# A first head pair projected side by side, and bias reads and stores issued by POOL

## The chip, the core and the metric

The kernel runs on one core of a Trainium2 chip. Five engines work side by side and wait for each other through semaphores: TensorE (PE in the profile; its weight loads are PEld), VectorE (DVE), ScalarE (ACT), GpSimd (POOL) and SyncE (SP). Transfers between main memory (DRAM) and the on-chip memory are issued by an engine's queue and carried out by 16 DMA engines that all queues share. The metric is device time in microseconds, median of several executions. Before the change it is 973.29 us (three runs, 971.8 to 973.51).

## The reference

One inference step of a two-layer encoder on 288 tokens at once: 256 of a prompt and 32 of a sample that has cached keys and values. The model width is 1024, everything is float32. Cut to its order:

```python
for layer in range(2):
    h = rmsnorm(x, g_mix[layer])
    if layer == 0:   # 16 heads of 64 from one projection
        qa, ka, va, qb, kb, vb = proj_ab(h, w_in_ab)
        o = merge_heads(chunk_band_attn(qa, ka, va, rel_bias_a),   # 8 heads, bias by clipped distance
                        stick_break(qb, kb, vb))                   # 8 heads, no softmax
    else:
        q, k, v, log_f = proj_c(h, w_in_c, b_f_c)                  # 16 heads
        o = forget_attn(q, k, v, log_f)                            # logits + cumulative log forget
    x = x + o @ w_out[layer]
    x = x + memory_attn(rmsnorm(x, g_xattn[layer]), *memory_kv(mem_prompt, ...), w_xq, w_xo)
    x = x + swiglu(rmsnorm(x, g_ffn[layer]), w_gate, w_up, w_down)
y = rmsnorm(x, g_final)
```

Besides y, the keys and values of both layers, those of the memory tokens and the log forget values are outputs. In the banded attention of layer 0 a frame reads its own chunk of 64 and the chunks before it; the bias of head h for query i and key j is a table entry at the distance i - j, clipped at 128.

## The kernel before

**Layout.** Activations lie transposed: eight blocks `x[k]` of 128 features by 288 tokens. Weights come in units of 128 x 1024 float32 (512 KB), one unit giving 128 output features: eight 128 x 128 blocks, one for each block of x. Each number is kept as a rounded part and a remainder (`hi`, `lo` for weights; `hh`, `hl` for activations), and `mm3` makes each product of three TensorE instructions, hi x hh, hi x hl and lo x hh. A unit's projection is thus 24 matrix products over 288 columns, summed in one PSUM bank.

**Units.** `unit(src)` (line 132) takes one of four buffers `st`, has SP load the unit, ScalarE copies it to `hi` (line 141) and VectorE subtracts to get `lo` (line 142). There are five buffers for `hi` and four for `lo`. `project` runs a unit's 24 products into a bank of tag `pj` (four banks, `acc`) and then calls `tick()`. Small work, attention above all, uses four further banks of tag `at` (`att`).

**Ticks.** Attention, norm scales and the preparation of memory tokens are generators in the list `active`. Each `tick()` lets each of them run to its next `yield`, so that their instructions stand between two projections. `Next.scale` has the columns of the norm (`Norm.columns`: sums of squares on TensorE, then eleven small VectorE instructions for the inverse root), a `yield`, and then the rows (`Norm.rows`: TensorE spreads the scale over the partitions, ScalarE copies it to `rstd`). A projection's result is multiplied by `rstd` when it leaves PSUM; projections that end before `rstd` is there hold their bank and wait in the list `waiting`.

**The start.** SP loads the first unit in three parts between the four pieces of x. ScalarE and VectorE scale and split each block of x by the gain (`split_scaled`, lines 247 and 250), and the first unit's products follow block by block. Keys and values are loaded as whole units. `pairs` then runs over eight head pairs: `proj(j)` projects queries, keys and values, the pair's attention is made active, after each second pair that of the sample too, and `memory.steps` puts projections of the memory tokens between.

**The bias of layer 0.** `rel_lines` makes a line of 384 biases per head, writes it to DRAM, and eight DRAM to DRAM copies (line 745) repeat it 128 times with a step of 385, so that a read with a step of 384 is the line shifted by one per row. `rel_prompt` reads two rectangles per head from this (lines 755 and 756), and POOL fills the masked corners. `softmax` adds the bias on VectorE (line 350); the transposes at lines 374 to 376 follow on TensorE. In layer 1 POOL builds the bias (lines 901 to 904) from the cumulative sums, which SP reads back from DRAM (`ck`, line 896).

**Orders.** A planner at compile time sets each engine's order from the order of the code and from when it expects operands to be ready; on the chip each engine then works strictly in that order and waits where an operand is late. SP issues every transfer: weights, x, bias reads, stores of keys and values (line 730), of memory keys (553) and values, of the forget values (848, 849) and of y (976).

## Time and profile before

| | |
|---|---|
| median of three runs | 973.29 us |
| the profiled execution | 974.15 us, of which 972.3 us are the span from first to last instruction |
| granted TensorE clock, mean | 0.995 |
| busy: TensorE, VectorE, ScalarE, POOL | 955.3, 588.6, 484.8, 195.1 us |
| matrix products on TensorE | 7495 |
| moved by DMA | 163.59 MB, 168 GB/s on the mean |

A row of a timeline gives the start and the length in microseconds, the engine, the line, the operation and what it writes and reads; in brackets stands how long the engine was idle before it and what ended that. `SPq` is SP's queue: the row tells when a transfer is issued, not when it lands. Rows of the chain of waits give start, length and what the end of the program hung on at that moment. A row of stretches gives, for a part of the span, each engine's busy time and number of instructions, the granted clock of TensorE and what the DMA engines did. Neighbouring matrix products overlap in the records, so that the distance of their starts, not their length, is what one costs.

### The profile page before, as it was taken

What the parts mean: (1) busy time and instruction counts of PE and PEld (TensorE: products, weight loads), DVE (VectorE), ACT (ScalarE), POOL (GpSimd) and SP (SyncE); (2) the same over time, 40 slices, a digit from 0 to 9 for tenths busy, and PEclk for the clock granted to TensorE, in tenths of its full rate; (3) what the DMA queues carried; (4) which work ended last, traced back from release to release, by engine and by line L of the source; (5) the groups of instructions that cost most, each with busy time, mean ns of one, the idle gap of its engine ahead of it and who ended that gap; (6) DMA issues with size and microseconds to landing.
All of it is one profiled execution on the core that took longest, in us unless ns stands there. A gap on an engine that the chain in (4) does not pass through costs nothing.

```text
span 972.3 us, 19122 instructions
## 1 busy us (share of the span) xinstructions
PE 955.3 (98%) x7495; PEld 923.2 (95%) x7495; DVE 588.6 (61%) x1133; ACT 484.8 (50%) x856; POOL 195.1 (20%) x291
## 2 busy tenths in 40 slices
PE   8999999999999999999999999999999999999997
PEld 7889999998999999999998999999989999999996
DVE  6587555676666555754565666657757655555452
ACT  5456768545554444444444545446546544444331
POOL 3021001310213222411004333213002222222010
PEclk9999999999999999999999999999999999999999
DMA  7775455544254444554555555555434444444431
GB/s 232 247 241 189 137 180 181 183 162 147 103 174 154 173 162 164 191 192 160 173 202 161 179 190 191 169 164 179 150 117 159 159 159 173 163 164 173 165 117 49
DMA packets 59721, 163.59 MB, mean 168 GB/s; under 512 B 8192, under 2 KB 20528, under 8 KB 59632
## 3 DMA queue, kind: packets, MB, share of 16 engines
q1 hardware_dynamic: 59632, 162.38, 49.0%
q8 instruction: 59, 0.97, 0.4%
q14 instruction: 30, 0.25, 0.1%
HBM read 152.20 MB, written 11.72 MB: 169 GB/s over the span
## 4 chain that ended last, share of the span: by engine, by line
PE 91%; DMA 3%; DVE 3%; issue 1%; ACT 1%; SPq 1%; POOL 0%; DVEq 0%; POOLq 0%; ACTq 0%
PE pj L68 51%; PE dn L68 14%; PE op L68 11%; PE mv L68 5%; PE po L68 1%; PE xo L68 1%; PE xs L68 1%; DMA st<-w_ab 1%; PE zb L68 1%; PE sc L68 1%; DVE lo L142 1%; DMA skew<-lined 1%; DMA x<-xT 1%; PE xss L68 1%; PE xt L614 0%
## 5 line engine op out<-in xcount | busy, mean ns | idle before, releaser
L141 ACT CAST hi<-st 128x1024 fp32r<-128x1024 f32 x260 | 272.2, 1049 | 335.7 <-issue 147.3
L68 PE MATMUL pj<-hh,hi 128*128 128x288 f32 (+1 forms) x1352 | 406.3, 301 | 0.0
L68 PE MATMUL pj<-hl,hi 128*128 128x288 f32 (+1 forms) x1352 | 399.9, 296 | 1.7 <-DVE hl L250 1.7
L68 PE MATMUL pj<-hh,lo 128*128 128x288 f32 (+1 forms) x1352 | 400.2, 296 | 0.0
L142 DVE TENSOR_TENSOR lo<-st,hi 128x1024 fp32r<-128x1024 f32 x260 | 322.7, 1242 | 127.4 <-PE dn L68 41.2
L68 PEld LDWEIGHTS pj<-hh,hi 128*128 128x128 f32 x1352 | 257.0, 190 | 5.8 <-issue 4.2
L68 PEld LDWEIGHTS pj<-hl,hi 128*128 128x128 f32 x1352 | 257.1, 190 | 3.3 <-DVE hl L250 3.2
L68 PEld LDWEIGHTS pj<-hh,lo 128*128 128x128 f32 x1352 | 256.9, 190 | 0.0
L68 PE MATMUL dn<-fh,hi 128*128 128x288 f32 x400 | 108.5, 294 | 0.0
L68 PE MATMUL dn<-fh,lo 128*128 128x288 f32 x352 | 103.3, 294 | 0.0
L68 PE MATMUL dn<-fl,hi 128*128 128x288 f32 x304 | 89.5, 294 | 0.0
L68 PE MATMUL op<-ol,hi 128*128 128x288 f32 x256 | 75.8, 297 | 0.0
L68 PE MATMUL op<-oh,hi 128*128 128x288 f32 x256 | 75.5, 297 | 0.0
L68 PE MATMUL op<-oh,lo 128*128 128x288 f32 x256 | 75.2, 294 | 0.0
L68 PEld LDWEIGHTS dn<-fh,hi 128*128 128x128 f32 x400 | 72.3, 188 | 0.0
L68 PEld LDWEIGHTS dn<-fh,lo 128*128 128x128 f32 x352 | 66.2, 188 | 0.0
L213 POOL TENSOR_TENSOR ssq<-ssq,sq 128x288 f32<-128x288 f32 (+1 forms) x37 | 37.7, 1018 | 119.8 <-ACT sq L202 76.8
L68 PEld LDWEIGHTS dn<-fl,hi 128*128 128x128 f32 x304 | 57.1, 188 | 0.0
L695 POOL TENSOR_TENSOR fl<-us,fh 128x288 fp32r<-128x288 f32 x38 | 32.9, 865 | 119.3 <-ACT fh L694 119.3
L690 DVE TENSOR_TENSOR us<-pj,rstd 128x288 f32<-128x288 f32 x44 | 20.1, 457 | 59.9 <-PE pj L68 59.9
L691 POOL TENSOR_TENSOR gs<-gs,sg 128x288 f32<-128x288 f32 x44 | 38.9, 884 | 75.8 <-ACT sg L689 75.8
L68 PEld LDWEIGHTS op<-ol,hi 128*128 128x128 f32 x256 | 48.2, 188 | 0.6 <-issue 0.4
(257 smaller groups left out, 1204.9 us busy)
## 6 DMA issues: line engine op xcount, KB each, us to landing
st<-w_gate SPq DMA_DIRECT2D x44, 512.0 KB, 3.3
st<-w_up SPq DMA_DIRECT2D x44, 512.0 KB, 3.2
st<-w_down SPq DMA_DIRECT2D x44, 512.0 KB, 3.2
st<-w_c SPq DMA_DIRECT2D x25, 512.0 KB, 3.3
st<-w_ab SPq DMA_DIRECT2D x23, 512.0 KB, 4.4
st<-w_xk SPq DMA_DIRECT2D x16, 512.0 KB, 3.4
st<-w_xv SPq DMA_DIRECT2D x16, 512.0 KB, 3.5
st<-w_xq SPq DMA_DIRECT2D x16, 512.0 KB, 3.5
```

Of the source, the lines that this page charges most:

```text
L68: T.matmul(out, lhsT, rhs, start=start, stop=stop, skip_group_check=True)
L141: S.copy(hi[:, b], st[:, b])
L142: V.tensor_tensor(lo[:, b], st[:, b], hi[:, b].bitcast(F32), ALU.subtract)
L213: eng.tensor_tensor(s[:, :self.n], self.acc[i][:, :self.n], q[:, :self.n], ALU.add)
L690: V.tensor_tensor(us, pu[:, :NT], cur.r, ALU.mult)
L691: G.tensor_tensor(gs, gs, sg, ALU.mult)
L695: G.tensor_tensor(lo, us, hi.bitcast(F32), ALU.subtract)
```

## The change

- The first pair's three units are loaded in parts (256, 256 and 512 columns), part by part between the pieces of x, and split into hi and lo as the parts arrive. `side_by_side` runs, for each block of x, the three products of queries, keys and values, into three banks (one of tag `at`, two of tag `pj`), and calls `tick()` once, where the three projections before called it three times.
- The columns of the first norm come at the first tick, right after those 72 products, and the rows two ticks later, after the second unit of pair 1. The first pair's attention in layer 0 is held back by two ticks, in layer 1 by one (`later`).
- POOL's queue issues what concerns the bias of layer 0 (the line, its copy to DRAM, the skew, the reads) and the stores of keys, values, memory keys, memory values and forget values. SP keeps the loads of weights, x, caches and memory tokens, the read back of the cumulative sums, and the store of y.
- The line is made at the start. The skewed copy has 64 rows a head for 128 and is written by two transfers of four heads for eight of one. The bias of a head is one tile of 128 x 256 for 128 x 384: the later query half has its keys 0 to 255, the earlier half uses columns 128 to 255, and one corner is masked. The tiles come from the general pool of token tiles, and a pair's reads are issued ahead of its projections.
- y is stored in three transfers for six.

```diff
-    first = wp.tile([P, 1024], F32, tag="st", bufs=4, name="first")
-    def first_part(c0, c1):
-        DMA.dma_start(first[:, c0:c1], a["w_ab"][0][:, c0:c1])
-    first_part(0, 256)
+    first = [wp.tile([P, 1024], F32, tag="st", bufs=4, name=f"first{i}") for i in range(3)]
+    def first_part(i, c0, c1):
+        DMA.dma_start(first[i][:, c0:c1], a["w_ab"][4 * i][:, c0:c1])
+    PARTS = ((0, 256), (256, 512), (512, 1024))
+    first_part(0, *PARTS[0])
     for i in range(4):
         DMA.dma_start(xh[i], a["xT"][:, 2 * i * NT:2 * (i + 1) * NT])
         if i == 0:
             DMA.dma_start(gain, a["gains"])
-            first_part(256, 512)
-        if i == 1:
-            first_part(512, 1024)
+        if i < 3:
+            for u in range(3):
+                if i or u:
+                    first_part(u, *PARTS[i])
...
+    SKEW = 64 * 385
+    line = cst.tile([8, 384], F32, name="line")
+    lined = dr.tile([8, 384], F32, name="lined")
+    skew = dr.tile([8, SKEW], F32, name="skew")
+    G.dma_start(line[:, 128:384], a["rel"][:, 0:256])
...
+    G.tensor_copy(line[:, 0:128], line[:, 128:129].to_broadcast([8, 128]))
+    G.dma_start(lined, line)
+    for h in range(0, 8, 4):
+        G.dma_start(bass.AP(tensor=skew.tensor, offset=skew.offset + h * SKEW, ap=[[SKEW, 4], [385, 64], [1, 384]]),
+                    bass.AP(tensor=lined.tensor, offset=lined.offset + 384 * h, ap=[[384, 4], [0, 64], [1, 384]]))
...
-    def unit(src, st=None, pieces=1):
-        if st is None:
-            st = wp.tile([P, 1024], F32, tag="st", bufs=4, name=name("st"))
-            DMA.dma_start(st, src)
-        hi = wp.tile([P, 1024], F32R, tag="hi", bufs=5, name=name("hi"))
-        lo = wp.tile([P, 1024], F32R, tag="lo", bufs=4, name=name("lo"))
-        for c in range(pieces):
-            b = slice(c * 1024 // pieces, (c + 1) * 1024 // pieces)
-            S.copy(hi[:, b], st[:, b])
-            V.tensor_tensor(lo[:, b], st[:, b], hi[:, b].bitcast(F32), ALU.subtract)
-        return hi, lo
+    def unit_tiles():
+        return [wp.tile([P, 1024], F32R, tag=t, bufs=n, name=name(t)) for t, n in (("hi", 5), ("lo", 4))]
+    def split_weights(st, w, c0=0, c1=1024):
+        hi, lo = (t[:, c0:c1] for t in w)
+        S.copy(hi, st[:, c0:c1])
+        V.tensor_tensor(lo, st[:, c0:c1], hi.bitcast(F32), ALU.subtract)
+    def unit(src):
+        st = wp.tile([P, 1024], F32, tag="st", bufs=4, name=name("st"))
+        DMA.dma_start(st, src)
+        w = unit_tiles()
+        split_weights(st, w)
+        return w
...
-    def project(src, h, n=NT, w=None, begun=None):
-        if begun:
-            w, p = begun
-        else:
-            w, p = w or unit(src), acc("pj")
-        with tc.issue_after(warmed.ins):
-            for k in range(BEGIN if begun else 0, KT):
-                mm3(p[:, :n], w, k, h, k, k == 0, k == KT - 1)
+    def project(src, h, n=NT, begun=None):
+        w, p = begun or (unit(src), acc("pj"))
+        for k in range(BEGIN if begun else 0, KT):
+            mm3(p[:, :n], w, k, h, k, k == 0, k == KT - 1)
         tick()
         return p
...
+    def store(dst, t):
+        G.dma_start(dst, t)
...
-            if self.gi != 1:
+            if self.gi > 1:
                 yield 1
             y = self.norm.columns()
             yield 1
+            if self.gi == 0:
+                yield 1
             p = self.norm.rows(y)
...
+                b0 = at[i] if at else c0
+                V.tensor_tensor_reduce(out=out[:, c0:c1], in0=s[:, c0:c1], in1=bias[:, b0:b0 + c1 - c0], scale=-1.0, scalar=3e38,
...
-                DMA.dma_start(a["mkT"][l, i], t[:, 0:NP])
+                store(a["mkT"][l, i], t[:, 0:NP])
...
-                        DMA.dma_start(a["mv"][l, t, :, hd * 256:hd * 256 + 256], v[:, 0:NP])
+                        store(a["mv"][l, t, :, hd * 256:hd * 256 + 256], v[:, 0:NP])
...
-    def rel_lines():
-        ln = cst.tile([8, 384], F32, name="line")
-        DMA.dma_start(ln[:, 128:384], a["rel"][:, 0:256])
-        V.tensor_copy(ln[:, 0:128], ln[:, 128:129].to_broadcast([8, 128]))
-        d = dr.tile([8, 384], F32, name="lined")
-        DMA.dma_start(d, ln)
-        sk = dr.tile([8, 128 * 385], F32, name="skew")
-        for h in range(8):
-            DMA.dma_start(bass.AP(tensor=sk.tensor, offset=sk.offset + h * 128 * 385, ap=[[385, P], [1, 384]]),
-                          bass.AP(tensor=d.tensor, offset=d.offset + 384 * h, ap=[[0, P], [1, 384]]))
-        return sk
-    def rel_rows(sk, h, c, rows, n):
-        return bass.AP(tensor=sk.tensor, offset=sk.offset + h * 128 * 385 + c, ap=[[384, rows], [1, n]])
-    def rel_prompt(sk, h):
-        t = wk.tile([P, 384], F32, tag="bi", bufs=5, name=name("bi"))
-        DMA.dma_start(t[:, 0:128], rel_rows(sk, h, 256, P, 128))
-        DMA.dma_start(t[:, 128:384], rel_rows(sk, h, 128, P, 256))
-        G.memset(t[0:64, 64:128], NEG)
-        G.memset(t[0:64, 320:384], NEG)
+    def rel_rows(h, c, rows, n):
+        return bass.AP(tensor=skew.tensor, offset=skew.offset + h * SKEW + c, ap=[[384, rows], [1, n]])
+    def rel_prompt(h):
+        t = tok("bi")
+        G.memset(t[0:64, 192:256], NEG)
+        G.dma_start(t[0:64, 0:192], rel_rows(h, 128, 64, 192))
+        G.dma_start(t[64:128, 0:256], rel_rows(h, 64, 64, 256))
         return t
 
-    def rel_sample(sk, g):
+    def rel_sample(g):
         t = wk.tile([P, 384], F32, tag="bi", bufs=5, name=name("bs"))
         for h in range(4):
-            DMA.dma_start(t[32 * h:32 * h + 32, 0:160], rel_rows(sk, 4 * g + h, 128, NS, 160))
+            G.dma_start(t[32 * h:32 * h + 32, 0:160], rel_rows(4 * g + h, 128, NS, 160))
...
+        def side_by_side():
+            p = [att("pj"), acc("pj"), acc("pj")]
+            with tc.issue_after(warmed.ins):
+                for k in range(KT):
+                    for u in range(3):
+                        mm3(p[u][:, :NT], w0[u], k, cur.h, k, k == 0, k == KT - 1)
+            tick()
+            return p
+        biases = {}
         def proj(j):
+            if j < 4:
+                biases[j] = [rel_prompt(2 * j + i) for i in range(2)]
             b = 12 * (j // 4) + j % 4
             kv = 8 * (j // 4) + j % 4
-            qs[j] = evac_q(cur, project(w[b], cur.h, w=w0 if j == 0 else None))
-            if j == 0:
-                proj.line = rel_lines()
-            ks[j] = evac_kv(cur, project(w[b + 4], cur.h), a["kv0"][kv])
-            vs[j] = evac_kv(cur, project(w[b + 8], cur.h), a["kv0"][kv + 4])
-        def attend(j):
+            p = side_by_side() if j == 0 else (project(w[b + 4 * i], cur.h) for i in range(3))
+            p = iter(p)
+            qs[j] = evac_q(cur, next(p))
+            ks[j] = evac_kv(cur, next(p), a["kv0"][kv])
+            vs[j] = evac_kv(cur, next(p), a["kv0"][kv + 4])
+        def attention(j):
             args = (qs[j], ks[j], vs[j], vns, j)
             if j < 4:
-                return attend_prompt(*args, [rel_prompt(proj.line, 2 * j + i) for i in range(2)], o[0][j], o[1][j])
+                return attend_prompt(*args, biases.pop(j), o[0][j], o[1][j], (128, 0))
             return stick_prompt(*args, o[0][j], o[1][j])
+        def attend(j):
+            return later(attention(j), 2) if j == 0 else attention(j)
...
+    def later(g, n):
+        for _ in range(n):
+            yield 1
+        yield from g
...
-        DMA.dma_start(a["lf"][0:256].rearrange("(t p) h -> p t h", p=P), lf[:, 0:32].rearrange("p (t h) -> p t h", h=H))
-        DMA.dma_start(a["lf"][256:288], lf[0:NS, 32:48])
+        G.dma_start(a["lf"][0:256].rearrange("(t p) h -> p t h", p=P), lf[:, 0:32].rearrange("p (t h) -> p t h", h=H))
+        G.dma_start(a["lf"][256:288], lf[0:NS, 32:48])
...
-            return attend_prompt(qs[j], ks[j], vs[j], vns, j, bias, o[0][j], o[1][j])
+            return later(attend_prompt(qs[j], ks[j], vs[j], vns, j, bias, o[0][j], o[1][j]), j == 0)
...
-    w0 = None
+    w0 = [unit_tiles() for _ in first]
     for m in range(KT):
         cur.block(m, start=True)
-        if m == 1:
-            w0 = unit(None, first, 4)
+        if m in (1, 3, 5):
+            for st, w in zip(first, w0):
+                split_weights(st, w, *PARTS[m // 2])
...
-            DMA.dma_start(a["y"][P * t:min(P * t + P, NT), b], out[r, b])
+        DMA.dma_start(a["y"][P * t:min(P * t + P, NT)], out[r])
```

11 lines of the change are left out of this document (5 added, 6 removed).

## The prediction

> **What bounds the kernel now.** I read the page first: the span and the engines' shares of it.
>
> ```profile
> span 972.3 us, 19122 instructions
> PE 955.3 (98%) x7495; PEld 923.2 (95%) x7495; DVE 588.6 (61%) x1133; ACT 484.8 (50%) x856; POOL 195.1 (20%) x291
> ```
>
> TensorE is the bound nearly everywhere, and the change removes none of its matrix products. So whatever it can win lies in the 17 us in which TensorE was idle and in the stretches in which it was busy but slow. Next I cut the span into stretches around its gaps; columns are length, then busy time and instruction count of PE, PEld, DVE, ACT and POOL, the granted clock, the DMA share and GB/s.
>
> ```profile
> 5.10:17.10 12.00, 10.30 (x36) 8.72 (x36) 10.91 (x20) 8.48 (x17) 4.82 (x6) 1.00 0.76 273
> 17.10:31.70 14.60, 14.60 (x115) 14.03 (x114) 7.04 (x19) 3.16 (x6) 1.17 (x8) 1.00 0.90 248
> 31.70:34.10 2.40, 0.38 (x4) 0.14 (x2) 2.15 (x12) 1.83 (x8) 0.00 (x0) 1.00 0.60 198
> 34.10:37.60 3.50, 3.48 (x16) 3.09 (x16) 1.52 (x5) 1.94 (x4) 0.00 (x0) 0.51 0.52 156
> 62.90:65.00 2.10, 1.19 (x7) 0.64 (x6) 2.10 (x8) 1.53 (x4) 0.80 (x1) 1.00 0.99 292
> 80.00:100.00 20.00, 19.88 (x172) 18.60 (x172) 12.99 (x31) 12.25 (x20) 2.91 (x2) 1.00 0.52 178
> 522.10:524.00 1.90, 0.20 (x3) 0.03 (x1) 1.19 (x7) 1.46 (x7) 0.89 (x3) 1.00 0.08 20
> 525.60:529.10 3.50, 3.50 (x17) 3.50 (x16) 0.78 (x1) 0.29 (x1) 0.00 (x0) 0.51 0.53 142
> ```
>
> A healthy stretch is 80 to 100: TensorE idle 0.12 us of 20. Against it stand four losses. The start: 12 us hold 36 products. Two idle gaps of 2.0 us (2.40 - 0.38) and 1.7 us (1.90 - 0.20), each followed by about 3.4 us at a granted clock of 0.5, in which half the work is done: another 1.7 us each. A smaller gap of 0.9 us (2.10 - 1.19) at 62.9. What a product costs shows in the starts of successive ones, early and late:
>
> ```profile
> 5.13 0.61 PE L68 MATMUL pj<-hh,hi 128*128 128x288 f32 x1
> 6.08 0.61 PE L68 MATMUL pj<-hl,hi 128*128 128x288 f32 x1 [0.34 <-DVE hl L250]
> 11.68 0.61 PE L68 MATMUL pj<-hl,hi 128*128 128x288 f32 x1 [1.08 <-DVE hl L250]
> ...
> 14.49 0.44 PE L68 MATMUL pj<-hh,hi 128*128 128x288 f32 x1
> 14.73 0.44 PE L68 MATMUL pj<-hl,hi 128*128 128x288 f32 x1
> ...
> 18.02 0.30 PE L68 MATMUL pj<-hh,hi 128*128 128x288 f32 x1
> 18.15 0.29 PE L68 MATMUL pj<-hl,hi 128*128 128x288 f32 x1
> ```
>
> They follow each other by 0.24 us in the first 17 us and by 0.13 us afterwards. Early TensorE is slow and also waits for x: the first product starts at 5.13, the second at 6.08.
>
> The gap at 31.7 I followed through the chain of waits, then through SP's and VectorE's timelines.
>
> ```profile
> 16.27 6.79 DMA skew<-lined
> 23.14 6.50 DMA st<-w_ab
> 39.73 0.84 PE po L68 x8
> ```
>
> ```profile
> 13.74 5.05 SPq L745 DMA_DIRECT2D skew<-lined  x8
> 22.72 0.32 SPq L756 DMA_DIRECT2D bi<-skew  x1
> 23.14 1.21 SPq L136 DMA_DIRECT2D st<-w_ab  x1
> ...
> 30.80 1.23 DVE L142 TENSOR_TENSOR lo<-st,hi 128x1024 fp32r<-128x1024 f32 x1 [2.97 <-ACT hi L141]
> 31.95 0.28 DVE L350 CUSTOM_DVE_ANT_0 e<-sc,bi 128x128 f32<-128x128 f32 x1
> ```
>
> SP issues in order. It spent 5.05 us on the eight skew copies; then the bias reads wait for those copies to land, and behind a bias read stands the next weight load, issued only at 23.14 and landed 6.50 later. ScalarE splits it, VectorE splits it at 30.80, and behind VectorE's split waits the softmax of the first pair (31.95), whose result the transposes on TensorE need at 31.7 and lack until 33.9. SP's order makes this gap, not bandwidth: SP waits while weights could flow.
>
> **The change, part by part.** The sum is made against the profiled execution, 974.15 us, 0.86 above the median of 973.29.
>
> First pair side by side. TensorE gets nine products per block of x in place of three while x arrives. Bytes: three weight units (1.57 MB), x (1.18 MB) and the gains are 2.8 MB, as much as is moved today by 13 us, only in another order:
>
> ```profile
> GB/s 0 0 0 0 0 19 186 203 173 269 358 286 256 79 53 131 232 275 366 352 336 347 314 339 288 311 336 440 439 410 416 416 403 303 189 63 25 0 0 0
> DMA packets 1456, 2.80 MB, mean 215 GB/s; under 512 B 296, under 2 KB 560, under 8 KB 1456
> ```
>
> So the last of x comes at about 12.5, or later with the skew copies beside it; I take 13.5. ScalarE, VectorE and SP do the same work cut finer (five more issues of 0.4 to 0.6 us, before x's last piece). TensorE: busy without gaps from 6.1 us. Today it turns fast at 17.0, 5.3 us after the last gap (before 11.68); with gapless work from 6.1, I let it turn at 11.0 (bounds 10 and never). That is some 23 products by 11.0 and 49 more at 0.13, thus 17.4; from the supply, 13.5 + 1.0 for the scaled copies + 18 x 0.13 = 16.8. I take 18.2 for the pair, 0.8 above the later of these because the second and third unit's first parts are split one after another while TensorE waits; bounds 17.2 and 22.7 (slow throughout: 6.1 + 69 x 0.24).
>
> Rows of the norm later. The order becomes pair 0, norm columns, two units of pair 1, norm rows, third unit. Prices:
>
> ```profile
> 18.82 1.40 PE L68 MATMUL nrm<-mean,ssq 128*128 128x2 f32 x12
> ...
> 23.33 0.75 PE L68 MATMUL nr<-ident,y 128*128 128x128 f32 x6
> ...
> 24.12 0.40 ACT L280 COPY rstd<-nr 128x288 f32<-128x288 f32 x1 [5.61 <-PE nr L68]
> 24.92 0.81 DVE L729 TENSOR_TENSOR kv<-pj,rstd 128x288 f32<-128x288 f32 x2
> ...
> 27.18 0.27 PE L332 MATMUL vt<-ident,kv 128*128 128x128 f32 x1
> 28.46 0.40 PE L68 MATMUL pj<-hh,hi 128*128 128x288 f32 x1
> ```
>
> Columns 1.4, rows 0.75. The third unit must wait for a bank: four "pj" banks hold k and v of pair 0 and two units of pair 1, and the first is free after the rows, the copy to rstd and two evacuations, the second of them the first of the two at 24.92 (0.45 each): about 25.3, 1.3 us after the rows end at 24.08. Queued behind this wait on TensorE is everything else; nothing hides it. It is the new stall. After: 18.2 + 1.4 + 48 x 0.13 + 0.75 + 1.3 + 24 x 0.13 = 31.0; the transposes of v with the scores (1.28, from 27.18 to 28.46) and the transposes of the weights (0.75) make 33.0. Today the same work stands done at 39.7 (39.73 in the chain above). Gain 6.7, bounds 2.2 (pair done at 22.7) and 7.7. The gap and slow clock at 31.7 are in it: skew and bias no longer pass SP, and weight loads run four buffers ahead.
>
> First attention two steps later. Its transposes and those of pair 1's values fall into one step and share four banks: a one-off loss of 0.7 (0 to 1.5; the copies that free a bank take 0.4 each).
>
> Bias reads and stores to POOL. Weight loads no longer queue behind them. The 0.9 at 62.9 has the same cause as the gap at 31.7 (softmax behind a late split): gain 0.9 (0 to 1). In layer 1:
>
> ```profile
> 513.51 2.28 SPq L553 DMA_DIRECT2D mkT<-mk  x2
> 515.89 0.38 SPq L896 DMA_DIRECT2D ck<-cumd  x1
> 520.10 0.40 POOL L901 TENSOR_TENSOR bc<-cumcol,ck 128x128 f32<-128x128 f32 x1 [3.35 <-DMA ck<-cumd]
> ```
>
> The read ck stood behind two stores of mk on SP, POOL built the bias only when it landed, and TensorE idled 1.7 us. After, ck has no store ahead, and the first attention comes one step (24 x 0.13 = 3.1 us) later: either alone covers 1.7, so gap and slow clock go: 3.5 (0 to 3.6).
>
> What POOL pays for an issue no row shows. Bounds by the nearest rows: SP's bias reads and a POOL elementwise operation.
>
> ```profile
> L755 SPq DMA_DIRECT2D bi<-skew x8: 320/357/454, 20.4 to 46.9; - x8
> L213 POOL TENSOR_TENSOR ssq<-ssq,sq 128x288 f32<-128x288 f32 (+1 forms) x37 | 37.7, 1018 | 119.8 <-ACT sq L202 76.8 <-issue 23.9 <-PE op L68 10.6
> L350 DVE CUSTOM_DVE_ANT_0 e<-sc,bi x16: 282/354/422, 31.9 to 75.2; 128x128 f32<-128x128 f32 x8, 128x256 f32<-128x256 f32 x8
> ```
>
> 0.36 to 1.0 us; an issue is likelier to resemble the longer, since POOL does it. 94 transfers move: 34 to 95 us beside 195 busy of 972. Layer 0's first four pairs need 36 of them by the last biased softmax at 75.2, 36 us from 60. It fits, and POOL's own operations (splits, norm sums) wait little: 0.5 loss (0 to 4).
>
> [...]
>
> Output in three stores for six.
>
> ```profile
> 966.70 3.07 SPq L976 DMA_DIRECT2D y<-yo  x6
> ```
>
> SP ends 3.07 us after the first issue; three issues would end at about 968.6, but the bytes stay: gain 0.5 (0 to 1.2).
>
> Sum: 6.7 - 0.7 + 0.9 + 3.5 - 0.5 + 0.5 = 10.4; 974.15 - 10.4 = 963.8, and against the median 962.9: **963 us**.
>
> **The rivals.** *The skew copies crowd the start.* Before, they begin at 13.7; now right after their 12 KB line is back, at about 8, with some 1.2 of the 2.8 MB still to move (the GB/s row up to there, 0.325 us a figure, gives 1.6). The copies are two with four heads outermost, and if these run on few of the 16 engines, x and weights wait there for the slowest share. Beside skew copies the engines moved 248 GB/s at a share of 0.90 (17.1 to 31.7) where the weights alone reach 416: 15.5 GB/s an engine, half of it for the weights. 1.2 MB/16 at 7.8 GB/s is 9.6 us, so x ends at 17.6, the pair at 21.0, and the gain is 2.8 smaller: 965.8. For it: the start's DMA share is already 0.76. Against: the copies carry half the bytes of before.
>
> [...]
>
> *The stall grows.* If the wait for the bank takes 2.1 us for 1.3, it has the length of the two gaps after which the clock halved: 0.8 + 1.7 lost, and 965.5. For it: ScalarE and VectorE run in order, and a split of 1.05 or 1.23 may stand before rstd or the evacuations. Against: the gap of 0.9 at 62.9 left the clock at 1.00.
>
> *It isn't side by side.* A planner sets the engines' orders; if it keeps unit after unit, only the gap and slow clock of 31.7 (3.7) remain of the 6.7: 966.
>
> *POOL is too slow (slower).* If an issue takes POOL 2.5 us, 36 of them take 90 us; from about 8 to 75.2 there are 67. The biases run 23 us late and TensorE waits: 963 + 23 = 986. Biases run late from 67/36 = 1.9 us an issue, and the kernel is slower than before from (67 + 10)/36 = 2.1. For it: POOL waits in order at each store. Against: that is twice the longer row.
>
> **How the numbers follow.** Forecast 0.54 (958 to 967), crowding 0.14, grown stall 0.10, not side by side 0.05, POOL too slow 0.11, and 0.06 that waits which I don't name take the gain back to within 0.2% (1.9 us, about what can be told from no change). Faster 0.83, same 0.06, slower 0.11. All gains at their upper ends give 960, and the stretch 40 to 80 may hold a few us more: low 956. With the start's gain at 2.2 (4.5 less) and layer 1's gap and slow clock kept (3.5), 963 + 8.0: high 971.
>
> **What would show it.** Right: the last product of pair 0 near 18; products 0.13 apart from about 11; no clock of 0.5 near 34 or 526; a gap of 1.3 after the norm's rows; SP issuing weights without waits for skew; POOL issues near 1 us. Wrong: POOL issues above 2 us, softmax waiting for bias reads, x ending after 16, a slow clock again after the norm's rows, or layer 1's first attention still waiting for its bias.

## The result: slower, and the profile after

| | median us | range | runs |
|---|---|---|---|
| before | 973.2 | 971.8 to 973.5 | 4 |
| changed | 985.7 | 985.6 to 986.8 | 4 |

The ratio is 1.0137, 95% interval 1.0123 to 1.0151: 12.5 us slower where 10.4 us faster was forecast. The profiled execution has a span of 984.0 us against 972.3. The head of its page:

```profile
span 984.0 us, 19160 instructions
...
PE 954.4 (97%) x7495; PEld 923.4 (94%) x7495; DVE 592.9 (60%) x1135; ACT 485.0 (49%) x859; POOL 250.6 (25%) x378
...
PEclk9699999999999999999999999999999999999999
```

TensorE's work is the same to the instruction (x7495) and its busy time too; it idles for 29.6 us (984.0 - 954.4) where it idled for 17.0. The place is read from one operation that both kernels have, on TensorE's timeline: the first transpose of the fifth pair's values, the first product of the gate in layer 1, and the transpose of layer 1's third pair. After:

```profile
99.51 0.28 PE L352 MATMUL vt<-ident,kv 128*128 128x128 f32 x1
...
522.22 0.39 PE L68 MATMUL gc<-tri,lf 128*16 128x256 f32 x1 [1.13 <-DVE lf L875]
...
561.35 0.27 PE L352 MATMUL vt<-ident,kv 128*128 128x128 f32 x1
```

And before:

```profile
86.04 0.28 PE L332 MATMUL vt<-ident,kv 128*128 128x128 f32 x1
...
508.89 0.39 PE L68 MATMUL gc<-tri,lf 128*16 128x256 f32 x1 [1.12 <-DVE lf L847]
...
550.52 0.27 PE L332 MATMUL vt<-ident,kv 128*128 128x128 f32 x1
```

At the fifth pair the changed kernel is 13.5 us behind, at the gate still 13.3, after layer 1's first pairs 10.8, at the end 11.7. So the first 86 us lose 13.5 where the prediction saw some 6.9 gained, layer 1's start gives back 2.5, the rest loses 0.9. The stretches of the start (columns as in the prediction), after and then before:

```profile
18.00:28.00 10.00, 8.08 (x60) 7.60 (x58) 4.96 (x3) 3.14 (x3) 7.40 (x10) 1.00 0.97 340
28.00:44.00 16.00, 3.76 (x16) 3.49 (x16) 7.75 (x22) 4.87 (x8) 6.26 (x17) 0.61 0.49 161
```

```profile
18.00:28.00 10.00, 10.00 (x83) 9.79 (x83) 5.24 (x18) 0.90 (x2) 0.59 (x4) 1.00 0.97 254
28.00:44.00 16.00, 13.96 (x95) 12.50 (x93) 7.94 (x22) 7.14 (x18) 0.58 (x4) 0.89 0.69 220
```

Between 28 and 44 us TensorE is busy 3.8 us of 16. Its timeline there says what it waits for:

```profile
27.25 0.83 PE L68 MATMUL nrm<-mean,ssq 128*128 128x2 f32 x6 [0.35 <-POOL ssq L231]
36.62 1.44 PE L68 MATMUL nrm<-mean,ssq 128*128 128x2 f32 x6 [8.54 <-DVE ssq L231]
40.32 1.49 PE L68 MATMUL nr<-ident,y 128*128 128x128 f32 x6 [2.27 <-DVE y L250]
43.25 0.58 PE L68 MATMUL pj<-hh,hi 128*128 128x288 f32 x1 [1.44 <-DVE kv L750]
```

The 72 products of the first pair are done at 18.5, and those of the second pair's queries and keys (q1, k1; v1 are its values, q2 the third pair's queries) at 26.9. Then the norm stops everything: the first half of its columns waits for POOL's sums, the second half 8.5 us for VectorE's, which wait for ScalarE's squares of x. The products behind the wait start 0.24 us apart (43.63, 43.87), the granted clock being 0.61 on the mean of this stretch. ScalarE's timeline, where x lay ready since 13.0:

```profile
29.90 1.04 ACT L152 CAST hi<-st 128x1024 fp32r<-128x1024 f32 x1 [2.78 <-DMA st<-w_ab]
...
33.23 1.04 ACT L152 CAST hi<-st 128x1024 fp32r<-128x1024 f32 x1 [0.81 <-DMA st<-w_ab]
34.18 1.44 ACT L220 ACTIVATE sq<-x 128x288 f32<-128x288 f32 x4
```

The planner has put the four squares behind the splits of seven later units (those that follow the first pair's three), and each split waits for its weights. Those are late: transfers issued between 12.9 and 22.7 us (first row) against all of this weight in the whole run (second), issue to landing:

```profile
st<-w_ab SPq DMA_DIRECT2D x2, 512.0 KB, 9.6
```

```profile
st<-w_ab SPq DMA_DIRECT2D x21, 512.0 KB, 3.7
```

POOL's half stands behind landings too:

```profile
5.78 0.55 POOL L130 DMA_DIRECT2D lined<-line  x1
11.38 1.73 POOL L132 DMA_DIRECT2D skew<-lined  x2 [5.05 <-DMA lined<-line]
13.12 2.02 POOL L218 TENSOR_TENSOR sq<-x 128x288 f32<-128x288 f32 x2
20.55 0.54 POOL L771 DMA_DIRECT2D bs<-skew  x1 [5.41 <-DMA skew<-lined]
21.11 0.82 POOL L231 TENSOR_TENSOR ssq<-sq,sq 128x288 f32<-128x288 f32 x1
```

Lined takes 5.3 us to land, the skew copies wait 5.05 for it with the squares behind them, and the first sum (21.11) stands behind a bias read that waits 5.41 us for skew.

### The profile page after: what moved, and what is told of

The parts are those of the page before. It is cut to its first block, busy times and chain, and to the rows that moved or that the text cites. A ratio compares the mean times of both kernels' runs of the same rounds, so it can differ in the third digit from the quotient of the medians.

```text
span 984.0 us, 19160 instructions
## 1 busy us (share of the span) xinstructions
PE 954.4 (97%) x7495; PEld 923.4 (94%) x7495; DVE 592.9 (60%) x1135; ACT 485.0 (49%) x859; POOL 250.6 (25%) x378
## 4 chain that ended last, share of the span: by engine, by line
PE 92%; DMA 3%; DVE 2%; ACT 1%; issue 1%; SPq 1%; DVEq 0%; ACTq 0%
PE pj L68 52%; PE dn L68 14%; PE op L68 10%; PE mv L68 5%; DMA st<-w_ab 2%; PE po L68 1%; PE xo L68 1%; PE sc L68 1%; PE zb L68 1%; PE xs L68 1%; PE nrm L68 1%; DMA first<-w_ab 1%; PE nr L68 1%; PE xss L68 1%; DVE lo L153 0%
## 5 line engine op out<-in xcount | busy, mean ns | idle before, releaser
L711 DVE TENSOR_TENSOR us<-pj,rstd 128x288 f32<-128x288 f32 x44 | 20.1, 457 | 58.6 <-PE pj L68 58.6
```

The costliest lines, as they stand in the source:

```text
L711: V.tensor_tensor(us, pu[:, :NT], cur.r, ALU.mult)
```

## The experiments

All are the changed kernel with one edit, or a combination of such edits; none leaves work out. Ratios are to the kernel before on the same chip, whose median is 972.0 to 973.2 us; a difference in us between two rows from different chips can be off by about as much as these differ. "Behind" is the start of the fifth pair's transposes against 86.04 us, from each profile.

| kernel | us | ratio, 95% | behind, us |
|---|---|---|---|
| changed | 985.7 | 1.0137 (1.0123 to 1.0151) | +13.5 |
| squares ahead of skew copies | 976.8 | 1.0043 (1.0028 to 1.0059) | +3.5 |
| eight copies by head | 977.5 | 1.0045 (1.0029 to 1.0060) | +5.0 |
| both of these | 980.2 | 1.0075 (1.0060 to 1.0090) | +8.7 |
| squares ahead of splits | 981.0 | 1.0092 (1.0072 to 1.0112) | +7.7 |
| both orders | 981.0 | 1.0078 (1.0056 to 1.0099) | +9.8 |
| both orders, caches later | 980.6 | 1.0073 (1.0056 to 1.0090) | +5.5 |
| issuers only | 975.2 | 1.0028 (1.0014 to 1.0042) | +3.1 |
| side by side only | 979.7 | 1.0073 (1.0056 to 1.0090) | +4.2 |
| chain on SP | 983.2 | 1.0110 (1.0095 to 1.0125) | +8.0 |
| chain on SP, rows outermost | 969.9 | 0.9978 (0.9968 to 0.9987) | -1.7 |
| the same, unit by unit | 972.1 | 0.9999 (0.9987 to 1.0010) | +0.6 |
| layer 1 not later | 986.6 | 1.0151 (1.0136 to 1.0167) | +15.4 |
| rows outermost, on POOL | 978.7 | 1.0068 (1.0051 to 1.0085) | +6.0 |
| chain on SP, stores behind | 979.3 | 1.0072 (1.0057 to 1.0088) | +4.8 |
| rows outermost, squares first | 968.7 | 0.9964 (0.9950 to 0.9978) | -4.5 |
| the same, sums before line | 966.6 | 0.9940 (0.9926 to 0.9953) | -5.8 |

"Layer 1 not later" leaves the start as it is in the changed kernel and still stands 2.0 us further behind there: differences below some 2 us in one profile's start tell nothing.

**First four: order or bandwidth.** The edit of the first, POOL's order (sums[True] is POOL's last sum of squares, sums[False] VectorE's, square ScalarE's last square; issue_after sets the order on the engine):

```diff
-    for h in range(0, 8, 4):
-        G.dma_start(bass.AP(tensor=skew.tensor, offset=skew.offset + h * SKEW, ap=[[SKEW, 4], [385, 64], [1, 384]]),
-                    bass.AP(tensor=lined.tensor, offset=lined.offset + 384 * h, ap=[[384, 4], [0, 64], [1, 384]]))
...
+    with tc.issue_after(cur.norm.sums[True].ins):
+        for h in range(0, 8, 4):
+            G.dma_start(bass.AP(tensor=skew.tensor, offset=skew.offset + h * SKEW, ap=[[SKEW, 4], [385, 64], [1, 384]]),
+                        bass.AP(tensor=lined.tensor, offset=lined.offset + 384 * h, ap=[[384, 4], [0, 64], [1, 384]]))
```

> The changed kernel (985.7), with one edit: the two skew copies, and with them all that POOL reads out of skew, are issued behind POOL's last sum of the squares of x. In the changed kernel POOL's squares of x began at 13.12 us, behind the wait for the landing of lined, and its last sum ended at 27.2, behind the wait for the landing of skew; with the edit both come right after x. With it the planner also puts ScalarE's four squares two splits earlier (they stand behind the split of k1 and of v1 only, in the changed kernel behind seven). The order theory (the norm is late because its squares and sums stand in the queues of POOL and ScalarE behind work that waits for landings): the columns begin at 19 to 24 instead of 27.3 and 36.6, the rows by 25 instead of 40.3, and about 13 of the 13.5 us that the start lost come back, less what late biases cost the first attention: 968 to 974 us. The bandwidth theory (the copies with four heads outermost and the 5 MB around them make the weights land late, whatever the order): the copies only run later, the weights still land as late as 20 to 26 us, and the splits with the squares behind them stay late: 980 us or more.

Of the second, the shape of the copies:

```diff
-    for h in range(0, 8, 4):
+    for h in range(8):
-        G.dma_start(bass.AP(tensor=skew.tensor, offset=skew.offset + h * SKEW, ap=[[SKEW, 4], [385, 64], [1, 384]]),
-                    bass.AP(tensor=lined.tensor, offset=lined.offset + 384 * h, ap=[[384, 4], [0, 64], [1, 384]]))
+        G.dma_start(bass.AP(tensor=skew.tensor, offset=skew.offset + h * SKEW, ap=[[385, 64], [1, 384]]),
+                    bass.AP(tensor=lined.tensor, offset=lined.offset + 384 * h, ap=[[0, 64], [1, 384]]))
```

> The changed kernel with one edit: the skew table is written by eight copies of one head, the 64 rows outermost, instead of two copies of four heads, the heads outermost; they stand at the same place of POOL's order. POOL still waits for the landing of lined (11.1 us), then issues eight at 0.55 us (estimate from the issues of the changed kernel), 4.4 us instead of 1.7, and its sums still stand between the reads of the sample's biases that wait for skew. The planner puts three of ScalarE's squares behind four splits and the last behind six. The bandwidth theory: the copies are done in 2 to 4 us instead of 9 to 11, the weights of k1, v1, q2 land 5 us sooner or more, the norm comes soon after: 970 us or less. The order theory: the norm still waits for POOL's sums, which end at some 20 to 24, and ScalarE's last square at some 25: a gain of only a part, 975 to 982 us.

The third is both edits.

> Both edits together: the skew copies behind POOL's last sum, and eight of them with the 64 rows outermost. The order theory: as with the copies moved alone, and a little better if the biases come sooner: 965 to 972 us, and within 3 us of the kernel with the move alone. The bandwidth theory: as with the shape alone, within 2 us of it. If each alone gives half and the two together all, both causes are needed.

The fourth, ScalarE's and VectorE's order:

```diff
-        split_weights(st, w)
+        if len(after_squares) < 8:
+            after_squares.append(src)
+            with tc.issue_after(first_norm[0].square.ins), tc.issue_after(first_norm[0].sums[False].ins):
+                split_weights(st, w)
+        else:
+            split_weights(st, w)
```

> The changed kernel with one edit: POOL's order and the skew copies stay, but the first eight splits of later units are issued behind ScalarE's four squares of x and VectorE's last sum. So ScalarE squares x right after the first pair's splits, at some 14 us instead of 34.18, and the second half of the norm no longer waits for late weights; POOL's last sum still ends at some 27. The order theory, with ScalarE's place as the larger half of the cost: columns at some 27, rows at some 31 instead of 40.3, 9 of the 13.5 us back: 976 us (974 to 979). If POOL's waits alone made the lateness: 983 or more. The bandwidth theory: the weights land as late as before, but the products of the later units also need the rows' bank only, so 980 us or more.

Measured 976.8, 977.5, 980.2 and 981.0. Each edit alone takes back 4.7 to 8.9 of 12.5 us, and the first two together 5.5, less than either: neither theory stands as it was put. The second run is where the order theory had it, the fourth where the bandwidth theory had it, the first and the third where neither had them. With POOL's order alone the columns start at 19.8 as expected, but the second half still waits 4.9 us for VectorE's sums.

**Both orders, and the caches.** The first and fourth edit together; then also the caches and the memory behind the fourth later unit's load on SP (newest is SP's last weight load, and sample creates its caches one step later):

```diff
+        with tc.issue_after(newest[0].ins):
-        DMA.dma_start(t, src)
+            DMA.dma_start(t, src)
...
-                DMA.dma_start(st, a["memT"][:, 1024 * c:1024 * c + 1024])
+                with tc.issue_after(newest[0].ins):
+                    DMA.dma_start(st, a["memT"][:, 1024 * c:1024 * c + 1024])
```

> Both orders at once: the skew copies and all reads of skew behind POOL's last sum, and ScalarE's four squares and VectorE's three sums ahead of the splits of all later units. Transfers, their shapes and SP's order stay. With one order alone the norm waited for the other engine (with the copies moved: 5.1 us for VectorE's sums at 25.3; with the squares moved: 3.7 us for POOL's sums at 24.3). The order theory: both halves of the columns run at some 20 us in one piece, the rows come 5 us sooner than with the copies moved alone (34.6), and the total falls by 4 to 5 from its 976.8: 971 to 973 us. The theory of late weights (from 8 to 33 us the transfer engines are busy nearly throughout; whatever order the computing engines have, the units of the second pair wait for weights that land at 20 to 29 us behind the skew copies and the caches): the norm is early and the units then wait for their weights instead: 975 us or more.

> Both orders as above, and besides the caches and the memory leave SP behind the load of the fourth later unit (q2) instead of ahead of it, the second pair of caches several units later still: 1 MB less between 14 and 30 us. The order theory: no difference from both orders alone, within 1.5 us. The theory of late weights: the weights of q2 and of the units behind it land some 3 us sooner, and the total falls by 1.5 to 4 us below that of both orders alone.

Measured 981.0 and 980.6: by the first of the two the order theory falls, which had 971 to 973. The 1 MB of caches is not the crowd either: without it q2's weights land at 26.1 instead of 30.7, and the total falls by 0.4 us, within the intervals, where the theory of late weights had 1.5 to 4. In the first of the two the columns run in one piece at 19.65, and the rows come at 34.82 none the less. VectorE's timeline between them:

```profile
26.19 0.16 DVE L250 TENSOR_SCALAR ms<-nrm 128x6 f32<-128x6 f32 x1
26.83 1.23 DVE L150 TENSOR_TENSOR lo<-st,hi 128x1024 fp32r<-128x1024 f32 x1 [0.48 <-ACT hi L149]
27.97 0.17 DVE L251 TENSOR_SCALAR y<-ms 128x6 int32<-128x6 int32 x1
31.87 1.23 DVE L150 TENSOR_TENSOR lo<-st,hi 128x1024 fp32r<-128x1024 f32 x1 [3.73 <-ACT hi L149]
33.01 0.15 DVE L253 TENSOR_TENSOR nt<-y 128x6 f32<-128x6 f32 x1
```

The norm's square root is a chain of eleven small steps (ms, y, nt), and the planner has put splits (lo) between them. Each split waits for a late weight, and the chain takes from 26.2 to 34.8. The same eleven steps run from 38.1 to 40.3 in the changed kernel, 2.2 us. So in these runs the norm is late where a late weight's split stands ahead of one of its steps.

**The two halves of the change apart.** Issuers only: POOL issues as in the changed kernel, but the first pair is unit by unit with rows and first attention where they were. Side by side only: every transfer that the change gave to POOL is SP's again. Of the first, and then of the second:

```diff
-            p = side_by_side() if j == 0 else (project(w[b + 4 * i], cur.h) for i in range(3))
+            p = (project(w[b + 4 * i], cur.h, w=w0 if i == j == 0 else None) for i in range(3))
...
-            return later(attention(j), 2) if j == 0 else attention(j)
+            return attention(j)
```

```diff
-        G.dma_start(dst, t)
+        DMA.dma_start(dst, t)
...
-    G.dma_start(lined, line)
+    DMA.dma_start(lined, line)
...
-        G.dma_start(t[0:64, 0:192], rel_rows(h, 128, 64, 192))
+        DMA.dma_start(t[0:64, 0:192], rel_rows(h, 128, 64, 192))
```

> The issuers alone: POOL issues the bias chain, the biases and the stores as in the changed kernel, with the early, smaller skew table; but the first pair is projected unit by unit, its weights are loaded as before the change, and the rows of the norm and the first attention come where they came before. If the issuers are a gain by themselves, as the prediction had it (gap at 62.9 us: 0.9; layer 1 with the clock behind it: 3.5; less 0.5 for POOL): 968 to 971 us. If POOL's waits and the early skew copies are what costs, whatever the projection: 976 us or more; the planner puts POOL's squares ahead of the skew copies here by itself, so that this much cannot come from POOL's order.

> The projection side by side alone, rows and first attention later with it: every transfer that the change gave to POOL (line, lined, skew, biases, stores of kv, mkT, mv and lf) is issued by SP again; the smaller skew table stays. SP's order then has the wait for lined behind two units' weights and the reads of skew, with their wait for its landing, behind three units' weights, ahead of the fourth's. ScalarE's squares stand behind the split of k1 and v1 only, POOL's behind nothing. If side by side is the gain that the prediction had (6.7 less 0.7 at the start): 966 to 969 us. If the later rows and the crowded start cost by themselves: no gain or a loss, 973 us or more.

Measured 975.2 and 979.7: each half loses by itself, the issuers a little less than the theory of POOL's waits had (976 or more). The issuers alone lose 3.1 us at the start, with the rows waiting 3.4 us for the same eleven steps on VectorE. Side by side alone is 4.5 us ahead of the kernel before at the second pair's transposes (39.3 against 43.8), and loses 8 by the third's, on SP:

```profile
31.15 4.38 SPq L197 DMA_DIRECT2D kv<-kv  x4
...
40.41 1.55 SPq L158 DMA_DIRECT2D st<-w_ab  x1
```

SP waits for skew with the bias reads (23.6) and for the norm's rows with the stores of kv (31.2); behind these and nine more reads the fourth later unit's weights leave at 40.4, in the changed kernel at 15.3. So side by side needs the other issuer for reads and stores; what POOL may have to give back is the bias chain (line, lined and the skew copies), which it issues ahead of the weights.

**The chain's place and shape.** Line, lined and skew on SP again (reads and stores stay on POOL); the same as one copy with the 64 rows outermost; and that with the first pair unit by unit. The edit of the second (the first keeps the loop, with DMA for G):

```diff
-    G.dma_start(line[:, 128:384], a["rel"][:, 0:256])
+    DMA.dma_start(line[:, 128:384], a["rel"][:, 0:256])
...
-    G.dma_start(lined, line)
+    DMA.dma_start(lined, line)
-    for h in range(0, 8, 4):
-        G.dma_start(bass.AP(tensor=skew.tensor, offset=skew.offset + h * SKEW, ap=[[SKEW, 4], [385, 64], [1, 384]]),
-                    bass.AP(tensor=lined.tensor, offset=lined.offset + 384 * h, ap=[[384, 4], [0, 64], [1, 384]]))
+    DMA.dma_start(bass.AP(tensor=skew.tensor, offset=skew.offset, ap=[[385, 64], [SKEW, 8], [1, 384]]),
+                  bass.AP(tensor=lined.tensor, offset=lined.offset, ap=[[0, 64], [384, 8], [1, 384]]))
```

> The changed kernel with the bias chain alone (line, lined, the two skew copies) issued by SP again; the reads of skew and the stores stay with POOL. SP's order then has the skew copies behind the loads of three later units (q1, k1, v1) and of a cache, and POOL's squares stand behind nothing. The theory left over from the runs so far: the weights of k1, v1 and q2 are late because the skew copies leave just ahead of them (issued at 11.4 to 12.3, the weights at 12.5 to 15.3, landed at 20 to 26), and the norm is late because its steps on POOL, ScalarE and VectorE stand in order behind splits of those weights. By it k1 lands at some 17 and v1 at 20, as where SP issued everything, the rows come at 29 or before, the first attention at 34 to 36, and SP, no longer held by the reads of skew and the stores of kv, has the next units' weights in time: 968 to 973 us. If the steps of the norm are late whatever the copies do: 976 us or more.

> As with the chain on SP, and the skew table written by one copy with the 64 rows outermost, then the heads, instead of two with four heads outermost. The theory that few engines carry a copy with four heads outermost: it lands in 3 to 5 us instead of 7 to 11, the weights behind it and the biases come sooner, 1 to 3 us less than with the chain on SP alone: 966 to 971 us. If the shape is no matter: the same within 1 us.

> The first pair unit by unit as before the change, the reads of skew and all stores on POOL, the chain on SP with the one copy with the rows outermost. Against the issuers alone (975.2) only the chain's place and shape differ. If the copies ahead of the weights were what made the issuers alone slower than the kernel before: 968 to 972 us, and the rest of the prediction's gains (0.9 at the gap, 2.4 in layer 1) shows. Otherwise 974 us or more.

Measured 983.2, 969.9 and 972.1. The chain's place alone, which was expected to do it, takes back 2.5 us (983.2, where 968 to 973 was expected); the shape then takes 13.4, where 1 to 3 was expected. Unit by unit comes out just above the 968 to 972 that the theory of place had. The windows of 16 to 24 us, four heads outermost and then rows outermost (the last two figures are the DMA share and GB/s):

```profile
16.00:18.00 2.00, 2.00 (x18) 2.00 (x17) 2.00 (x4) 1.16 (x3) 1.92 (x3) 1.00 0.94 306
18.00:20.50 2.50, 1.25 (x11) 1.02 (x9) 2.40 (x3) 1.66 (x3) 2.42 (x6) 1.00 0.40 130
20.50:24.00 3.50, 3.45 (x27) 3.37 (x28) 3.31 (x8) 0.00 (x0) 0.13 (x2) 1.00 0.86 277
```

```profile
16.00:18.00 2.00, 1.86 (x14) 1.60 (x12) 2.00 (x2) 1.32 (x3) 1.92 (x3) 1.00 0.93 317
18.00:20.50 2.50, 0.59 (x6) 0.39 (x4) 2.29 (x4) 1.45 (x3) 2.33 (x6) 1.00 0.96 276
20.50:24.00 3.50, 3.50 (x17) 3.50 (x18) 3.07 (x6) 0.00 (x0) 0.66 (x1) 0.51 1.03 371
```

With four heads outermost the sixteen engines are 40% busy from 18.0 to 20.5 and move 130 GB/s; with rows outermost 96% and 276. Counted over the packets in the trace, the copies with four heads outermost have exactly four packets in flight for 6.5 of the 9.1 us in which their packets run (18.2 to 27.4); the one copy has ten or more in flight for 2.7 of its 5.2 us and is done by 22.7. That agrees with the rival of the prediction that let these copies run on few of the sixteen engines. From SP the two copies together have hardly ever more than five packets in flight, as if both shared four engines; which engine carried a packet is not shown. From POOL the two copies overlap otherwise: with the squares ahead of them eight packets are in flight for 1.9 of 8.5 us, the most time at any number; in the changed kernel it is four, for 2.8 of 10.0 us, and up to ten at times.

Part of the 13.4 us could be the planner's: with four heads outermost it also put POOL's stores of kv ahead of the bias reads. Two runs tell these apart, the second with the one copy issued by POOL at the place that the change gave it. The edit of the first (newest is POOL's last bias read):

```diff
-        G.dma_start(dst, t)
+        with tc.issue_after(newest[0].ins):
+            G.dma_start(dst, t)
```

> The chain on SP as two copies with four heads outermost (983.2), and POOL's stores of kv put behind the first four bias reads. If the 13.4 us between this chain and the one copy came from POOL's order: 970 to 974 us. If from the transfer that runs on four engines until 27.4 us: 978 us or more. In between if both have a part.

> The changed kernel with the skew table written by one copy with the 64 rows outermost; POOL issues it at the place of the two. The planner then leaves no bias read between POOL's sums, and puts ScalarE's squares behind the splits of q1 and k1 only. If the shape is the larger cause: 970 to 975 us. If the place ahead of the weights of k1, v1 and q2 is: those land at 18 to 24 still, and it stays at 976 to 979, like the eight copies by head (977.5).

Measured 979.3 and 978.7: the first where the theory of four engines had it, the second where that of the place had it. With the stores behind the reads, four heads outermost cost 9.4 us (979.3 - 969.9) and POOL's order about 4 (983.2 - 979.3). On POOL the good shape saves 7.0 (985.7 - 978.7), and the place, with what the planner makes of it, costs 8.8 (978.7 - 969.9; with four heads outermost 6.4, 985.7 - 979.3): there the copy leaves at 11.0, ahead of the weights of k1 and v1, which leave at 13.2 and 14.3 and land at 19.5 and 20.7; from SP it leaves at 15.8 behind them, and they land at 16.7 and 18.4.

**Layer 1's later step**, undone:

```diff
-            return later(attend_prompt(qs[j], ks[j], vs[j], vns, j, bias, o[0][j], o[1][j]), j == 0)
+            return attend_prompt(qs[j], ks[j], vs[j], vns, j, bias, o[0][j], o[1][j])
```

> The changed kernel with layer 1's first attention where it was before (not one step later); the issuers stay. In the changed kernel the stretch from the gate to the second pair of layer 1 is 2.45 us shorter than before. If the later step made this: 988.2 us. If the issuer of lf (POOL instead of SP, so that ck is no longer behind stores) made it: 985.7 us, the same. A word on the start: it is untouched, and this run also tells how far the stretch up to pair 4 varies from one build to the next with nothing changed there.

Measured 986.6, 0.9 more than the changed kernel, less than its start alone differs by. The stretch from the gate to the third pair is 3.1 us shorter than before without the later step, and 2.5 with it. The row that answers to 520.10 of before, and SP's read ahead of it:

```profile
528.80 0.43 SPq L924 DMA_DIRECT2D ck<-cumd  x1
...
532.76 0.40 POOL L929 TENSOR_TENSOR bc<-cumcol,ck 128x128 f32<-128x128 f32 x1 [0.66 <-DMA ck<-cumd]
```

POOL builds the bias 8.6 us after the gate (524.2), not 11.2, because ck no longer stands behind stores on SP. TensorE waits 0.15 us at the first pair's transposes there, where before waited 1.70: the issuers alone close this gap. The later step alone closes it too: in side by side only, which has that step but SP's stores, the wait is 0.27 us. That run's stretch is still no shorter (+4.1 at the gate, +4.5 behind): in its profiled execution half the clock from 515.3 to 518.7 and a wait of 1.34 us for the sample's softmax at 543.8 take the gain back. In the profiles of the runs with POOL's stores the stretch is 0.7 to 3.1 us shorter than before; the two lowest (0.7 and 0.8) also have half the clock for 3.4 us behind the gate; why only some runs have that is not shown.

**A version that beats both.** The one copy on SP, with the norm's parts put ahead of what waits for late transfers: first ScalarE's squares and VectorE's sums (the fourth edit), then POOL's sums too, with the skew copy behind lined as above:

```diff
+    with tc.issue_after(cur.norm.sums[True].ins):
+        G.tensor_copy(line[:, 0:128], line[:, 128:129].to_broadcast([8, 128]))
+    DMA.dma_start(lined, line)
```

> The one copy with the rows outermost on SP (969.9), and ScalarE's four squares and VectorE's three sums ahead of the splits of later units. POOL's sums still end at about 20, because POOL's copy of line waits for line (13.1) ahead of them. The order theory: VectorE's half no longer matters, POOL's sets the columns at 19 to 20: a gain of 0 to 1.5, 968.5 to 970 us.

> As before it, and POOL's copy of line, with the rest of the chain, behind POOL's sums. POOL squares x as it arrives and ends at 15 to 17, so the columns follow pair 0 without a gap (18 us), the clock stays up, and k1's products run at 0.13 us: 3 to 4 us less than the one copy alone: 965 to 967.5 us. The rival: the skew table leaves and lands later, the first softmax waits for its bias: 970 us or more.

Measured 968.7 and 966.6, both times as expected, though the columns of the first come at 21.2 and not at 19 to 20. The last is 0.9940 of before, 0.9926 to 0.9953. On POOL, the last sum and the first bias read, and on TensorE, columns and rows:

```profile
10.10 0.89 POOL L234 TENSOR_TENSOR ssq<-ssq,sq 128x288 f32<-128x288 f32 x1
...
25.88 0.71 POOL L767 DMA_DIRECT2D bi<-skew  x1 [10.98 <-DMA skew<-lined]
```

```profile
18.30 1.40 PE L68 MATMUL nrm<-mean,ssq 128*128 128x2 f32 x12
...
26.35 0.85 PE L68 MATMUL nr<-ident,y 128*128 128x128 f32 x6 [0.20 <-DVE y L253]
28.64 0.37 PE L68 MATMUL pj<-hh,hi 128*128 128x288 f32 x1 [1.44 <-ACT hi L147]
...
29.26 0.44 PE L68 MATMUL pj<-hh,hi 128*128 128x288 f32 x1
29.50 0.44 PE L68 MATMUL pj<-hl,hi 128*128 128x288 f32 x1
```

And its two stretches, as above:

```profile
18.00:28.00 10.00, 9.00 (x70) 8.65 (x68) 5.72 (x16) 2.85 (x4) 2.12 (x4) 1.00 1.04 347
28.00:44.00 16.00, 15.36 (x119) 14.04 (x121) 12.75 (x43) 10.90 (x31) 10.72 (x23) 0.89 0.86 278
```

POOL's sums are done at 11.0, the columns follow pair 0 without a gap, the rows come at 26.4, and TensorE is busy 15.4 us of the 16 that held 3.8. What is left is the stall behind the rows: TensorE idles 1.44 us and then runs at half the clock from 28.9 to 32.3, with products 0.24 us apart, which costs it another 1.7 us (half of 3.4). With the weights on time, both orders take 3.3 us off 969.9 (the skew copy also leaves later with them, at 18.2 for 15.8, behind q2's load); with the weights late they left the start 9.8 us behind.

## Why the prediction was wrong, by its steps

- **First pair side by side: right.** Done at 18.5 for 18.2; x ended at 13.0 for 13.5; products were 0.13 us apart from 7.7 us, earlier than 11.0.
- **Rows of the norm later: this step failed.** "After: 18.2 + 1.4 + 48 x 0.13 + 0.75 + 1.3 + 24 x 0.13" lets the columns start when the products end. It priced the norm's work on TensorE and not its supply: squares, sums and the eleven steps on three engines, in order behind what waits for landings: splits of weights on ScalarE and VectorE, the bias chain on POOL. It also took for granted that those weights come ("weight loads run four buffers ahead"). They don't: three of the four buffers hold the first pair's weights until their last parts are split, so k1's and v1's loads leave only at 12.5 and 13.6, behind the skew copies, and land at 20.2 and 22.1. The columns came 18 us late in their second half. The stall behind the rows was as long as forecast (1.44 us idle for 1.3) and is in the best version too, but it is not all: there the clock halved behind it, as the rival "The stall grows" had it, though that put the length for this at 2.1 us. The forecast counted the idle time alone.
- **"POOL's own operations (splits, norm sums) wait little: 0.5 loss (0 to 4)": failed.** An issue costs POOL what was bounded, 0.52 us, as the row below has it, and POOL's busy time rose by 55 us (195.1 to 250.6) where 34 to 95 was given. But POOL waits in order for landings, 5.05 us for lined and 5.41 for skew, with the norm's sums behind.

```profile
L764 POOL DMA_DIRECT2D bi<-skew x8: 521/526/542, 28.7 to 72.4; - x8
```

- **Rival "the skew copies crowd the start": right cause, wrong victim, too small.** It let x wait (2.8 us); x was in by then, and the weights of the next units waited. Shape and place together are 15.8 us (985.7 - 969.9), where the rival had 2.8.
- **Rival "POOL is too slow" gave 986** and 985.7 came, but by luck: its issues take 0.52 us, far below the 2.5 that it supposed.
- **First attention later, gap at 62.9:** the best version shows the start's sum was near where the supply holds: 5.8 us gained at the fifth pair for 6.7 - 0.7 + 0.9 = 6.9. This compares single profiles, and that of before is of an execution of 974.15 us, slower than its medians. By medians the best version gains 5.4 us (972.0 - 966.6), about half of the 10.4. The stretch from third to fourth pair is 1.3 us shorter in the changed kernel (0.9 forecast).
- **Layer 1: mechanism right, size off.** 2.5 for 3.5. "Either alone covers 1.7" holds: 0.15 us of the wait are left with the issuers alone, 0.27 with the later step alone and with both. Two such waits in the changed kernel's stretch, 0.27 and 0.56 us, are part of the 1.0 that is missing.
- **Output in three stores: no gain.** SP ends 1.64 us after the first store's issue instead of 3.07, and from the last norm to the end it takes 11.2 us instead of 11.0.
- **Side by side itself is worth 2.3 us** (969.9 against 972.1) while the columns still come some two late (20.1 for 18.3 in the best version); unit by unit the other issuers gained nothing in all.

Left open: how much of a weight's late landing is its share on the engines that carry the copies, and how much the bytes in all. The changed kernel's trace records the landing of k1's load in sixteen updates of a semaphore: twelve come from 16.06 to 17.42 us, the last four from 19.81 to 20.16, and its split starts at 20.18. Which engines the late four belong to is not shown. How far the place alone counts, apart from the orders that the planner makes around it, was not taken apart either.

## What to carry to other kernels

When an engine gets work "earlier", list everything that the work's inputs stand behind in each in-order queue, and for each of those what it waits for: a weight that is late delays any small step that the planner has put behind its split (the norm's eleven steps took 8.6 us here in place of 2.2). Put a copy's long dimension outermost (64 rows for four heads saved 7.0 and 9.4 us here), and let a bulk copy leave behind the loads that are needed sooner, not ahead of them (6.4 and 8.8 us here, with what the planner made of it). Put the waits for round trips through memory on a queue whose followers can wait (5.05 us for lined and 5.41 for skew on POOL here).

## What the hardware showed beyond that

The same skew copies went out in different packets from the two issuers: from SP (chain on SP) 512 of 1,536 bytes, from POOL (changed kernel) 168 of 4,608, 8 of 1,536 and 504 of 12 bytes (counted in the traces, over both copies). Twelve kilobytes (lined) issued at 5.78 beside x and the weights took 5.3 us to land. And in the chain on SP, right behind the two copies with four heads outermost, SP's next two issues took 1.46 and 1.24 us, where the same kinds had taken 0.42 and 0.33 (with the stores behind: 1.41 and 1.39; behind the one copy 0.60 and 0.42):

```profile
13.63 0.33 SPq L158 DMA_DIRECT2D st<-w_ab  x1
14.01 0.42 SPq L527 DMA_DIRECT2D ca<-cab  x1
...
17.18 1.46 SPq L527 DMA_DIRECT2D ca<-cab  x1
18.74 1.24 SPq L158 DMA_DIRECT2D st<-w_ab  x1
```
